# Regrouping a scan's chunks and re-issuing its transfers in a one-core hybrid decoder layer

## The chip, the core and the metric

The kernel runs on one core of a Trainium2 chip. Its time is the device time of one launch, in microseconds (us). A core has five engines with instruction streams of their own: TensorE (PE) for matmuls, VectorE (DVE), ScalarE (ACT), GpSimd (POOL) and SyncE (SP). SP, ACT and POOL also issue DMA transfers, in the order of their own streams.

## What is computed

One layer for two groups of tokens that share all weights: a prompt of 512 tokens and 8 sample tokens with caches of 2048 tokens, 520 columns in all. All data are 32-bit floats.

```python
x = x + 0.5 * swiglu_1(rmsnorm(x))                 # widths 1024, 2816
h = rmsnorm(x); u, q, k, v, ga, gb = split(h @ w_in)
# branch A: diagonal complex state space model, 64 groups of 16 channels, 64 states each
state[t] = abar * state[t-1] + bbar * u[t]         # chunked over time; samples: one step
y = gelu(Re(C state) + D * u); y_a = y * sigmoid(y @ w_glu)
# branch B: 3 groups of 4 heads, windows (128, 512, 2048), dilations (1, 4, 16), QK-norm, ALiBi,
#           groups mixed by their softmax denominators; samples attend to the caches
x = x + (sigmoid(ga) * (y_a @ w_proj_a) + sigmoid(gb) * (o_b @ w_proj_b)) @ w_out
x = x + 0.5 * swiglu_2(rmsnorm(x))
# results: x, the last states, and the key/value buffers moved on by one token
```

## The kernel before

Activations are kept transposed: a tile holds 128 channels by 520 tokens. Each product block multiplies one 128-column slice of a weight by all eight activation tiles. Operands are split into a high and a low part (`wsplit`, L165: ACT makes `wh`, DVE makes `wl`), and three products of the parts are summed, in two halves of 260 columns: 48 matmuls per block in `mm` (L212), all recorded at L221. Weights come one block at a time through `wfetch` (L169) from SP's queue into two raw buffers, three blocks ahead.

The layer runs as: first SwiGLU (bank ring `bigA`), the projection `w_in` as 42 blocks (ring `bigB`, two pairs of PSUM banks), eight GLU blocks, the output projections, second SwiGLU. The 42 blocks are two q/k blocks, eight u blocks, ten q/k blocks, six v blocks, sixteen gate blocks. Other work is threaded between them by generators. `pace()` (L746) is called after every block from the seventh u block on, counts them in `n`, takes steps of the scan in proportion (`SC` per block), and takes one step of each other generator when `n` reaches the next number in its list: `LV` leave, `NB` norms, `AT` attention, `KS` sample scores, `SM` samples, `YB` y blocks. Gate blocks are n = 19 to 34 and GLU blocks 35 to 42. The tool that places instructions also reorders within an engine by its own model of time; matmuls marked by `mark` keep their order.

The state space model treats four tokens as one column of a chunk. An u block is evicted by DVE with the norm factor (L797, L799) into `us`, stored to DRAM `uD` in four transfers (L802), and loaded back as `ut` (L648) with groups on the partitions. `entry` (L669) multiplies `ut` by the matrices `mp` (from DRAM `pD`, L662) into the chunk sums `XS` (ACT, L677), one quarter in each quarter of a product block, from the fourth u block on. `scan` (L684) then runs over `XS` in two halves of the groups. There are 128 columns in time order, 16 blocks of 8: a first pass sums each block over its 8 places, a second carries the state over the 16 blocks one after the other, a third fills the places. A step (`advance`) is four DVE operations, L701 to L704, on 512 elements per partition in the first and third pass and on 32 in the second. `leave` (L757) multiplies the states by output matrices (`qD`, and `ut` again), evicts them (ACT, L767) and stores `yD` from SP (L774). `y_block` (L1043) loads y back and makes the gelu with ACT and DVE in turn.

Norm factors of q and k are stored to `hD` and spread over partitions by SP (L850) for DVE's `normalise` (L852). `scores` (L1069) loads keys and a query row for each sample into one buffer, `spare`, which is taken out of the ring of three matrix buffers `mts`.

Of the kernel before, what the change touches and what calls it, by code (L numbers as in the profile page):

```python
# [21 lines left out]
NT = 520  # L22
# [17 lines left out]
EARLY = 2  # L40
ENTER = 2
RB = 7


SC = 1.85
LV = (21, 22, 22, 24, 25, 25, 26, 26)
NB = (16, 17, 17, 17, 18, 18, 19, 20, 21, 22, 22, 22, 22)
AT = (23, 24, 26, 27, 27, 28, 28, 29, 29, 30, 30, 31, 31, 31, 32, 32, 33, 35, 37)
KS = (22, 23, 23, 24, 26, 26, 27, 28)
SM = (31, 31, 36, 39, 39)  # L50
YB = (29, 29, 29, 29, 29, 31, 31, 33)
NL = 12
KV = 8
# [5 lines left out]
def build(tc, A):  # L59
# [575 lines left out]
    ssm = ExitStack()  # L635
    smp = pool(ssm, "smp")
    NH = NP // 2
    XS = [smp.tile([128, 2, NH, 145], F32, name=f"XS{h}") for h in range(2)]
    x0 = tmp("G")[:, 0:NP * 16].rearrange("p (r x) -> p r x", r=2)
    for ri, n in enumerate(("x0_re", "x0_im")):  # L640
        dma(x0[:, ri], A[n])
    for h in range(2):
        S.activation(XS[h][:, :, :, 0:8], x0.rearrange("p r (a b) -> p r a b", b=8)[:, :, h * NH:(h + 1) * NH], AF.Copy)
        V.memset(XS[h][:, :, :, 8:9], 0.0)

    def uload(u):
# [22 lines left out]
    def entry():  # L669
        for u in range(NP // 4):  # L670
            ut, mp = uload(u), mload(pD, u, dma)
            for a in range(4):
                p = u * 4 + a
                ps = bank()
                for ri in range(2):
                    mark(T.matmul(ps[:, ri], lhsT=mp[:, a * 2 + ri], rhs=ut[:, a, 8:CW], start=True, stop=True))  # L676
                S.activation(XS[p // NH][:, :, p % NH, 9:145], ps[:, 0:2], AF.Copy)  # L677
                yield
# [5 lines left out]
    def scan(h):  # L684
        X, pr = XS[h], slice(h * NH, (h + 1) * NH)
        sums = smp.tile([128, 2, NH, 16], F32, name="sums", tag="sums", bufs=2)

        def swap(x):
            return bass.AP(tensor=x.tensor, offset=x.offset + x.ap[1][0],
                           ap=[list(x.ap[0]), [-x.ap[1][0], 2]] + [list(d) for d in x.ap[2:]])  # L690

        def advance(out, W, x, add):
            n = 1 if len(x.shape) == 3 else x.shape[3]
            t1, t2 = (tmp(t)[:, 0:2 * NH * n] for t in "ST")
            w = [c[:, :, pr] for c in W]
            if n == 1:
                t1, t2 = (t.rearrange("p (r a) -> p r a", r=2) for t in (t1, t2))
            else:
                w = [c.unsqueeze(3).broadcast_to([128, 2, NH, n]) for c in w]
                t1, t2 = (t.rearrange("p (r a b) -> p r a b", r=2, b=n) for t in (t1, t2))  # L700
            V.tensor_tensor(t1, w[0], x, ALU.mult)  # L701
            V.tensor_tensor(t2, w[1], swap(x), ALU.mult)  # L702
            V.tensor_tensor(t1, t1, t2, ALU.add)
            V.tensor_tensor(out, add, t1, ALU.add)  # L704

        def at(j):
            return X[:, :, :, 8 + j:8 + j + 121:8]

        for j in range(1, 8):
            advance(sums, W4, sums if j > 1 else at(1), at(1 + j))  # L710
            yield
        for b in range(16):
            advance(X[:, :, :, 16 + 8 * b], W32, X[:, :, :, 8 + 8 * b], sums[:, :, :, b])
            if b % 2:
                yield
        for j in range(7):
            advance(at(j + 1), W4, at(j), at(j + 1))
            yield

        x0 = [X[:, ri, :, 0:8] for ri in range(2)]  # L720
        xn = [X[:, ri, :, 137:145] for ri in range(2)]
        t = tmp("S")[:, 0:8 * NH].rearrange("p (a b) -> p a b", b=8)
        ab = lambda ri: A1[:, ri, pr].unsqueeze(2).broadcast_to([128, NH, 8])
# [3 lines left out]
        o = tmp("G")[:, 0:18 * NH].rearrange("p (r a b) -> p r a b", r=2, b=9)  # L727
        S.activation(o, X[:, :, :, 136:145], AF.Copy)
        for ri in range(2):
            later(A["ostate"][ri][:, pr], o[:, ri])  # L730
        yield


    def scans():
        lo, hi = scan(0), scan(1)
        for order in ((lo,) * 7, (lo, hi) * 8, (lo, hi) * 7 + (hi,), (lo,), (hi,) * 8):
            for x in order:
                next(x, None)
                yield
# [6 lines left out]
    def pace(n=1):  # L746
        paced["n"] += n
        while paced["s"] < paced["n"] * SC:
            next(scanning, None)
            paced["s"] += 1  # L750
        for at, it in side:
            while at and at[0] <= paced["n"]:
                at.pop(0)
                next(it)


    def leave():  # L757
        for u in range(NP // 4):
            mt, ut, ps = mload(qD, u, later), uload(u), big()
            X, p0 = XS[u * 4 // NH], u * 4 % NH  # L760
            for a in range(4):
                p = p0 + a
                out = ps[:, a // 2, a % 2 * NC:(a % 2 + 1) * NC]
                mark(T.matmul(out, lhsT=mt[:, a * 3], rhs=X[:, 0, p, 0:NC], start=True, stop=False))
                mark(T.matmul(out, lhsT=mt[:, a * 3 + 1], rhs=X[:, 1, p, 0:NC], start=False, stop=False))
                mark(T.matmul(out, lhsT=mt[:, a * 3 + 2], rhs=ut[:, a, 0:NC], start=False, stop=True))
            S.activation(X[:, 0, p0:p0 + 4, 0:NC].rearrange("p (x a) b -> p x a b", x=2),  # L767
                         ps[:, :, 0:2 * NC].rearrange("p x (a b) -> p x a b", b=NC), AF.Copy)
            if u % 2 == 1:
                p = u * 4 - 4  # L770
                for g2 in range(2):
                    for t in range(4):
                        r0 = g2 * 64 + t * 16
                        dma(yD[p:p + 8, g2, :, t].rearrange("a k j -> k a j"), X[r0:r0 + 16, 0, p0 - 4:p0 + 4, 0:NC])  # L774
            yield
# [8 lines left out]
    for m in range(KB):  # L784
        ps = big()
        mm(ps, wnext(), n2.xs, between=entering if m > ENTER else None)
        u = us.next()

        for hf, c0, c1 in ((0, 0, 256), (0, 256, 260), (1, 260, 384), (1, 384, 512)):
            o = u[:, c0 // 128:(c1 + 127) // 128, 8 + c0 % 128:8 + (c1 - 1) % 128 + 1]  # L790
            src = ps[:, hf, c0 - hf * H:c1 - hf * H]
            r = R2[:, c0:c1]
            if c1 - c0 > 128:
                src, r = (x.rearrange("p (a b) -> p a b", b=128) for x in (src, r))
            else:
                o = o[:, 0]
            V.tensor_tensor(o, src, r, ALU.mult)  # L797
        for o in (u[:, 0, 0:8], u[:, 3, NC:CW]):
            V.tensor_tensor(o, ps[:, 1, 512 - H:520 - H], R2[:, 512:520], ALU.mult)  # L799
        for s in range(4):  # L800
            o = uD[m]
            dma(bass.AP(tensor=o.tensor, offset=o.offset + s * 16 * 4 * CW, ap=[[64 * 4 * CW, 2], [CW, 64], [1, CW]]), u[:, s])  # L802
        if m > 5:
            pace()
# [4 lines left out]
    def columns():  # L809
        for r in range(4):  # L810
            later(Rt[r * 32:r * 32 + 32, 0:4], rD[1, r * 128:r * 128 + 128].rearrange("(i a) -> a i", a=32))
        later(Rt[:, 4:8], rD[1, 0:512].rearrange("(r n) -> n r", r=4))

    for b in range(2, 12):
        qk_block(b, entering)
        if b == RB:
            with behind(qk[b]):
                columns()
        pace()
# [28 lines left out]
    def spread(b):  # L848
        for x in range(2):
            dma(norms[b % 2][x * 64:x * 64 + 64], hD[2 * b + x:2 * b + x + 1].broadcast_to([64, NT]))  # L850

# [204 lines left out]

    spare = mts.tiles.pop().rearrange("p a b -> p (a b)")
    sc = atp.tile([128, 3, 8, 4], F32, name="sc")
# [97 lines left out]

    side.append((list(AT), attending))
    side.append((list(KS), scores()))
    side.append((list(SM), samples()))
    yout = outputs()  # L1160
    for i in range(16):
        gate(i)
        if i == NL:
            assert not side[0][0] and next(scanning, None) is None and not side[3][0]
# [195 lines left out]
```

## Time and profile before

| | |
|---|---|
| median of three runs | 1318.41 us (1314.51 to 1320.13) |
| the profiled execution | 1321.28 us |
| its span, first to last instruction | 1319.5 us |
| busy in the span: PE, DVE, ACT, POOL | 96%, 56%, 33%, 8% |

The rows below come from the profiled execution and its times count from the start of its span. PE rows that pack together matmuls of one line show how many by "x". "Idle before" is the time for which an engine did nothing ahead of an instruction, and after the arrow stands what ended it, as far as the profile can tell.

### The profile page before, as it was taken

The numbers are of one execution on the slowest core, as the hardware profiler recorded it, in microseconds if no ns is written. First come the engines' busy times: TensorE is split into PE (matmuls) and PEld (weight loads), VectorE is DVE, ScalarE is ACT, GpSimd is POOL, SyncE is SP. The second block draws the span as 40 slices with busy tenths as digits, with TensorE's granted clock in tenths as the row PEclk, the third lists the DMA queues.
The fourth block names the chain that finished last, engine by engine and source line by source line (L and its number), as shares of the span: only waits on it lengthen the run. The fifth ranks groups of instructions, "written<-read, shape, count | busy, mean of one in ns | idle before, by whom it ended". The sixth has DMA issues, their size and how long they took to land.

```text
span 1319.5 us, 25222 instructions
## 1 busy us (share of the span) xinstructions
PE 1273.0 (96%) x10575; PEld 1245.5 (94%) x10575; DVE 739.3 (56%) x1268; ACT 430.8 (33%) x677; POOL 109.0 (8%) x211
## 2 busy tenths in 40 slices
PE   8999999999999878996989999999999999999999
PEld 7999999999999878996988899999999999999998
DVE  6794454535564238998944666775544334443442
ACT  5332232223343222332243653443332222222220
POOL 0110000000103001001330220000010000000000
PEclk9999999999999898998989899999999999999999
DMA  6674365546655445226786534556564426433332
GB/s 216 216 228 158 95 240 190 148 150 204 200 164 171 125 124 140 81 82 200 236 250 199 169 97 147 166 161 206 165 255 156 152 93 224 160 96 112 120 101 85
DMA packets 97401, 213.88 MB, mean 162 GB/s; under 512 B 37076, under 2 KB 53232, under 8 KB 96520
## 3 DMA queue, kind: packets, MB, share of 16 engines
q1 hardware_dynamic: 79096, 145.90, 36.2%
q0 software_dynamic: 7184, 60.01, 13.0%
q10 hardware_dynamic: 11008, 6.36, 1.8%
q8 instruction: 83, 1.36, 0.4%
q14 instruction: 30, 0.25, 0.1%
HBM read 188.72 MB, written 68.60 MB: 195 GB/s over the span
## 4 chain that ended last, share of the span: by engine, by line
PE 81%; DMA 8%; DVE 5%; issue 2%; SPq 2%; ACT 1%; POOL 0%; DVEq 0%; ACTq 0%; POOLq 0%
PE bigB L221 38%; PE bigA L221 28%; PE third L221 12%; DMA mt<-qkD 2%; DMA wr<-in_win 1%; DVE wl L167 1%; PE s L676 1%; DMA OB<-hD 1%; DMA uD<-us 1%; PE sb L953 1%; PE s L982 1%; DMA vt<-wD 1%; DVE t_T L702 1%; DMA mt<-in_kv 1%; DVE mt L1074 1%
## 5 line engine op out<-in xcount | busy, mean ns | idle before, releaser
L166 ACT ACTIVATE wh<-wr 128x1024 fp32r<-128x1024 f32 (+3 forms) x212 | 214.3, 1011 | 581.0 <-PE bigB L221 205.1
L167 DVE TENSOR_TENSOR wl<-wr,wh 128x1024 fp32r<-128x1024 f32 (+3 forms) x212 | 246.1, 1161 | 55.2 <-ACT wh L166 53.6
L221 PE MATMUL bigB<-xh,wh 128*128 128x260 f32 (+1 forms) x1216 | 254.4, 290 | 4.0 <-DVE us L799 3.7
L221 PE MATMUL bigB<-xl,wh 128*128 128x260 f32 (+1 forms) x1216 | 253.8, 288 | 0.4 <-DVE xl L302 0.4
L221 PE MATMUL bigB<-xh,wl 128*128 128x260 f32 (+1 forms) x1216 | 249.6, 286 | 0.0
L221 PEld LDWEIGHTS bigB<-xh,wh 128*128 128x128 f32 x1216 | 191.5, 192 | 6.1 <-DVE us L799 3.9
L221 PEld LDWEIGHTS bigB<-xl,wh 128*128 128x128 f32 x1216 | 192.1, 192 | 3.8 <-issue 3.2
L221 PEld LDWEIGHTS bigB<-xh,wl 128*128 128x128 f32 x1216 | 191.2, 192 | 0.7 <-issue 0.7
L221 PE MATMUL bigA<-xh,wh 128*128 128x260 f32 x704 | 143.4, 285 | 2.0 <-ACT xh L257 1.2
L221 PE MATMUL bigA<-xl,wh 128*128 128x260 f32 x704 | 142.7, 284 | 0.6 <-DVE xl L258 0.6
L221 PE MATMUL bigA<-xh,wl 128*128 128x260 f32 x704 | 142.2, 284 | 0.5 <-DVE wl L167 0.5
L221 PEld LDWEIGHTS bigA<-xh,wh 128*128 128x128 f32 x704 | 109.2, 190 | 4.3 <-ACT xh L257 2.9
L221 PEld LDWEIGHTS bigA<-xl,wh 128*128 128x128 f32 x704 | 108.8, 189 | 1.6 <-DVE xl L258 1.6
L221 PEld LDWEIGHTS bigA<-xh,wl 128*128 128x128 f32 x704 | 109.0, 189 | 0.7 <-DVE wl L167 0.7
L120 POOL COPY pace<-ah 1x1 f32<-1x1 f32 x48 | 19.9, 416 | 768.8 <-ACT ah L301 768.8
L221 PE MATMUL bigA<-ah,wh 128*128 128x260 f32 x352 | 71.2, 283 | 0.0
L221 PE MATMUL bigA<-al,wh 128*128 128x260 f32 x352 | 71.0, 283 | 0.0
L221 PE MATMUL bigA<-ah,wl 128*128 128x260 f32 x352 | 70.6, 282 | 0.0
L221 PE MATMUL third<-xh,wh 128*128 128x260 f32 x288 | 58.0, 282 | 0.0
L221 PE MATMUL third<-xh,wl 128*128 128x260 f32 x288 | 57.9, 283 | 0.0
L221 PE MATMUL third<-xl,wh 128*128 128x260 f32 x288 | 57.8, 282 | 0.0
L221 PEld LDWEIGHTS bigA<-ah,wh 128*128 128x128 f32 x352 | 54.2, 189 | 0.1
(386 smaller groups left out, 2045.6 us busy)
## 6 DMA issues: line engine op xcount, KB each, us to landing
out_okv<-in_kv POOLq DMA_DIRECT2D x32, 1023.5 KB, 6.2
wr<-in_wg SPq DMA_DIRECT2D x43, 512.0 KB
wr<-in_wu SPq DMA_DIRECT2D x43, 512.0 KB
wr<-in_win SPq DMA_DIRECT2D x42, 512.0 KB
wr<-in_wd SPq DMA_DIRECT2D x32, 448.0 KB
wr<-in_wd SPq DMA_DIRECT2D x16, 512.0 KB
out_okv<-in_kv POOLq DMA_DIRECT2D x8, 1022.0 KB, 6.0
ut<-uD POOLq DMA_DIRECT2D x16, 288.0 KB, 5.4
```

The costliest lines, as they stand in the source:

```text
L120: ins = G.tensor_copy(pace[0:1, 0:1], t[0:1, 0:1])
L166: S.activation(h, raw, AF.Copy)
L167: V.tensor_tensor(l, raw, h, ALU.subtract)
L221: i = T.matmul(ps[:, hf, 0:x.shape[1]], lhsT=a[:, c], rhs=x, start=k == 0 and j == 0, stop=k == n - 1 and j == 2)
L676: mark(T.matmul(ps[:, ri], lhsT=mp[:, a * 2 + ri], rhs=ut[:, a, 8:CW], start=True, stop=True))
L702: V.tensor_tensor(t2, w[1], swap(x), ALU.mult)
L953: T.matmul(o, lhsT=q[pr, qc], rhs=k[pr, kc], start=True, stop=True)
L982: T.matmul(po[x * 64:x * 64 + 64, l * 128:l * 128 + 128], lhsT=vt[:, kt, c:c + 64], rhs=pTs[x][:, j], start=j in (j0, 2), stop=j % 2 == 1)
L1074: V.tensor_tensor(qb, qb, kt, ALU.mult)
```

## The change

The 128 columns of `XS` are stored by place in the block instead of in time order, so that the 16 blocks' values of one place lie side by side; u is written to `us` in that order, and leave's eviction puts it back into time order. The scan uses one set of temporary tiles per half, its two halves alternate over other stretches, and both halves' end states are stored together afterwards (`states`, from SP). u's stores move from SP to POOL, the entry matrices from SP to ACT, the norm spreads and y's stores from SP to POOL, the token factors `Rt` from POOL to SP. Entry starts one u block later. The u products are cut at column 256. Scores use the rotating buffers `kvt`, as the samples do, and start only when the scan's memory has been given back, which comes two gates earlier. leave keeps all three matrix buffers. All lists of `pace` are new.

```diff
-ENTER = 2
+ENTER = 3
-SC = 1.85
-LV = (21, 22, 22, 24, 25, 25, 26, 26)
-NB = (16, 17, 17, 17, 18, 18, 19, 20, 21, 22, 22, 22, 22)
-AT = (23, 24, 26, 27, 27, 28, 28, 29, 29, 30, 30, 31, 31, 31, 32, 32, 33, 35, 37)
-KS = (22, 23, 23, 24, 26, 26, 27, 28)
-SM = (31, 31, 36, 39, 39)
-YB = (29, 29, 29, 29, 29, 31, 31, 33)
-NL = 12
+SC = 1.9
+LV = (21, 21, 22, 22, 27, 27, 28, 28)
+NB = (15, 15, 16, 16, 17, 17, 18, 18, 19, 19, 20, 20, 24)
+AT = (25, 26, 27, 28, 29, 30, 31, 32, 32, 33, 34, 34, 35, 35, 36, 36, 37, 38, 40)
+KS = (29, 30, 30, 31, 31, 32, 32, 33)
+SM = (34, 34, 37, 39, 40)
+YB = (29, 29, 30, 30, 31, 31, 32, 33)
+NL = 10
...
-    XS = [smp.tile([128, 2, NH, 145], F32, name=f"XS{h}") for h in range(2)]
+    XS = [smp.tile([128, 2, NH, 160], F32, name=f"XS{h}") for h in range(2)]
...
-            ut, mp = uload(u), mload(pD, u, dma)
+            ut, mp = uload(u), mload(pD, u, put)
...
-                S.activation(XS[p // NH][:, :, p % NH, 9:145], ps[:, 0:2], AF.Copy)
+                S.activation(X[:, :, i, 24:160], ps[:, 0:2], AF.Copy)
...
-        sums = smp.tile([128, 2, NH, 16], F32, name="sums", tag="sums", bufs=2)
+        sums, u1, u2 = (tmp(t)[:, 0:32 * n].rearrange("p (r a b) -> p r a b", r=2, b=16) for t in "GST")
...
         def at(j):
-            return X[:, :, :, 8 + j:8 + j + 121:8]
+            return X[:, :, :, 8 + 16 * j:24 + 16 * j]
         for j in range(1, 8):
-            advance(sums, W4, sums if j > 1 else at(1), at(1 + j))
+            advance(sums if j < 7 else at(8), W4, sums if j > 1 else at(1), at(1 + j))
             yield
         for b in range(16):
-            advance(X[:, :, :, 16 + 8 * b], W32, X[:, :, :, 8 + 8 * b], sums[:, :, :, b])
+            out = X[:, :, :, 9 + b] if b < 15 else X[:, :, :, 151]
+            advance(out, W32, X[:, :, :, 8 + b], X[:, :, :, 136 + b])
...
+    def states():
+        for h in range(2):
+            o = tmp("G")[:, 0:18 * NH].rearrange("p (r a b) -> p r a b", r=2, b=9)
+            S.activation(o, XS[h][:, :, :, 151:160], AF.Copy)
+            for ri in range(2):
+                dma(A["ostate"][ri][:, h * NH:(h + 1) * NH], o[:, ri])
...
-        for order in ((lo,) * 7, (lo, hi) * 8, (lo, hi) * 7 + (hi,), (lo,), (hi,) * 8):
+        for order in ((lo,) * 11, (lo, hi) * 12, (hi,) * 11):
...
-        while paced["s"] < paced["n"] * SC:
+        while paced["s"] < (paced["n"] - 1) * SC:
...
-            S.activation(X[:, 0, p0:p0 + 4, 0:NC].rearrange("p (x a) b -> p x a b", x=2),
-                         ps[:, :, 0:2 * NC].rearrange("p x (a b) -> p x a b", b=NC), AF.Copy)
+            for x in range(2):
+                o, r = X[:, 0, p0 + 2 * x:p0 + 2 * x + 2, 0:NC], ps[:, x, 0:2 * NC].rearrange("p (a b) -> p a b", b=NC)
+                S.activation(o[:, :, 8:NC].rearrange("p a (b j) -> p a b j", j=8),
+                             r[:, :, 8:NC].rearrange("p a (j b) -> p a b j", j=8), AF.Copy)
+            S.activation(X[:, 0, p0:p0 + 4, 0:8].rearrange("p (x a) b -> p x a b", x=2),
+                         ps[:, :, 0:2 * NC].rearrange("p x (a b) -> p x a b", b=NC)[:, :, :, 0:8], AF.Copy)
...
-                        dma(yD[p:p + 8, g2, :, t].rearrange("a k j -> k a j"), X[r0:r0 + 16, 0, p0 - 4:p0 + 4, 0:NC])
+                        later(yD[p:p + 8, g2, :, t].rearrange("a k j -> k a j"), X[r0:r0 + 16, 0, p0 - 4:p0 + 4, 0:NC])
...
-        mm(ps, wnext(), n2.xs, between=entering if m > ENTER else None)
+        mm(ps, wnext(), n2.xs, cut=256, between=entering if m > ENTER else None)
...
-            V.tensor_tensor(o, src, r, ALU.mult)
+        for sg in range(4):
+            V.tensor_tensor(u[:, sg, 8:NC].rearrange("p (j b) -> p b j", j=8),
+                            *(x.rearrange("p (b j) -> p b j", j=8) for x in
+                              (ps[:, sg // 2, sg % 2 * 128:sg % 2 * 128 + 128], R2[:, sg * 128:sg * 128 + 128])), ALU.mult)
...
-            dma(bass.AP(tensor=o.tensor, offset=o.offset + s * 16 * 4 * CW, ap=[[64 * 4 * CW, 2], [CW, 64], [1, CW]]), u[:, s])
+            later(bass.AP(tensor=o.tensor, offset=o.offset + s * 16 * 4 * CW, ap=[[64 * 4 * CW, 2], [CW, 64], [1, CW]]), u[:, s])
...
-            with behind(qk[b]):
-                columns()
+            columns()
...
-            dma(norms[b % 2][x * 64:x * 64 + 64], hD[2 * b + x:2 * b + x + 1].broadcast_to([64, NT]))
+            later(norms[b % 2][x * 64:x * 64 + 64], hD[2 * b + x:2 * b + x + 1].broadcast_to([64, NT]))
...
-    spare = mts.tiles.pop().rearrange("p a b -> p (a b)")
...
-            kt, qb = spare[:, 0:768], spare[:, 768:1536]
+            kt, qb = (sap.tile([128, 768], F32, name="kvt", tag="kvt", bufs=KV) for _ in range(2))
...
-    side.append((list(KS), scores()))
-    side.append((list(SM), samples()))
...
+            states()
             ssm.close()
...
+            side.append((list(KS), scores()))
+            side.append((list(SM), samples()))
             side.append((list(YB), yout))
```

## Rows read from the trace of the kernel before

**Rows 1.** The page's slices: 40 equal parts of the span, tenths busy or granted.
```profile
PE   8999999999999878996989999999999999999999
...
DVE  6794454535564238998944666775544334443442
...
PEclk9999999999999898998989899999999999999999
```

**Rows 2.** Windows: us, busy us per engine (instructions), PEclk, DMA share, GB/s.
```profile
428.00:520.00 92.00, 73.23 (x548) 71.26 (x547) 38.52 (x81) 22.91 (x44) 6.42 (x11) 0.89 0.45 127
...
520.00:606.00 86.00, 86.00 (x747) 83.09 (x746) 83.14 (x207) 32.41 (x63) 5.13 (x9) 1.00 0.31 92
606.00:618.00 12.00, 1.60 (x12) 1.39 (x11) 9.32 (x22) 0.96 (x5) 0.76 (x1) 0.71 0.79 264
618.00:730.00 112.00, 102.78 (x795) 96.14 (x794) 74.26 (x117) 39.57 (x84) 27.52 (x45) 0.94 0.75 223
730.00:840.00 110.00, 109.53 (x907) 101.32 (x906) 73.18 (x119) 57.70 (x117) 14.08 (x24) 0.97 0.48 141
840.00:1319.00 479.00, 476.22 (x3982) 475.67 (x3980) 218.90 (x277) 136.17 (x170) 19.30 (x46) 1.00 0.45 151
```

**Rows 3.** Timeline of PE, instructions that waited: start, us, what, idle before.
```profile
434.81 1.25 PE L676 MATMUL s<-ut,mt 128*128 128x136 f32 x4 [3.45 <-issue]
...
617.40 0.41 PE L886 MATMUL s<-ident,OB 128*48 128x128 f32 x1 [10.40 <-DVE OB L927]
```

**Rows 4.** Timeline of POOL, two loads.
```profile
448.80 0.54 POOL L648 DMA_DIRECT2D ut<-uD  x1 [9.29 <-DMA uD<-us]
...
505.72 1.53 POOL L662 DMA_DIRECT2D mt<-qD  x2
```

**Rows 5.** Chain of waits, 428 to 530 us: start, us, what.
```profile
447.06 0.46 PE s L676 x4
...
447.53 1.44 PE bigB L221 x12
...
482.64 8.46 DMA uD<-us
```

**Rows 6.** Timeline of SP's queue, one turn and the start of the next.
```profile
444.90 6.99 SPq L802 DMA_DIRECT2D uD<-us  x4
451.99 2.45 SPq L175 DMA_DIRECT2D wr<-in_win  x1
454.49 1.32 SPq L662 DMA_DIRECT2D mt<-pD  x2
455.91 7.58 SPq L802 DMA_DIRECT2D uD<-us  x4
```

**Rows 7.** DMA issues by line: queue, count, KB each, median us to landing.
```profile
ut<-uD POOLq DMA_DIRECT2D x16, 288.0 KB, 5.4
```

**Rows 8.** Line L544: ns min/median/max, first and last start, forms.
```profile
L544 ACTq DMA_DIRECT2D pD<-pst x32: 582/628/3950, 110.3 to 369.1; - x32
```

**Rows 9.** DVE groups, 398 to 850 us: busy us, mean ns | idle before.
```profile
L167 DVE TENSOR_TENSOR wl<-wr,wh 128x1024 fp32r<-128x1024 f32 x51 | 62.2, 1220 | 19.1 <-ACT wh L166 19.0
...
L703 DVE TENSOR_TENSOR t_S<-t_S,t_T 128x512 f32<-128x512 f32 x28 | 19.3, 689 | 0.2
...
L701 DVE TENSOR_TENSOR t_S<-W,XS 128x512 f32<-128x512 f32 x16 | 18.4, 1148 | 0.0
...
L704 DVE TENSOR_TENSOR XS<-XS,t_S 128x512 f32<-128x512 f32 x14 | 16.2, 1156 | 0.0
...
L1074 DVE TENSOR_TENSOR mt<-mt 128x768 f32<-128x768 f32 x8 | 7.7, 958 | 29.6 <-DMA mt<-qkD 22.0 <-DMA yD<-XS 7.6
...
L1050 DVE TENSOR_SCALAR t_T<-t_T 128x520 f32<-128x520 f32 x8 | 3.7, 462 | 9.9 <-ACT t_T L1049 9.9
```

**Rows 10.** Timeline of DVE, the memset of nq.
```profile
491.29 0.17 DVE L822 MEMSET nq<- 128x130 f32 x1 [14.13 <-DMA uD<-us]
```

**Rows 11.** ACT groups, 398 to 850 us: leave eviction.
```profile
L767 ACT ACTIVATE XS<-bigB 128x544 f32<-128x544 f32 x8 | 5.0, 620 | 10.5 <-PE bigB L766 8.2 <-DMA yD<-XS 2.4
```

More of the change, by code (lines that the diff above doesn't have):

```diff
@@ L644, in build, with place @@
         V.memset(XS[h][:, :, :, 8:9], 0.0)
+    def place(p):
+        return XS[p // NH], p % NH
     def uload(u):
@@ L676, in entry @@
                     mark(T.matmul(ps[:, ri], lhsT=mp[:, a * 2 + ri], rhs=ut[:, a, 8:CW], start=True, stop=True))
-                S.activation(XS[p // NH][:, :, p % NH, 9:145], ps[:, 0:2], AF.Copy)
+                X, i = place(p)
+                S.activation(X[:, :, i, 24:160], ps[:, 0:2], AF.Copy)
                 yield
@@ L684, in scan @@
     def scan(h):
-        X, pr = XS[h], slice(h * NH, (h + 1) * NH)
-        sums = smp.tile([128, 2, NH, 16], F32, name="sums", tag="sums", bufs=2)
+        X, n, pr = XS[h], NH, slice(h * NH, (h + 1) * NH)
+        sums, u1, u2 = (tmp(t)[:, 0:32 * n].rearrange("p (r a b) -> p r a b", r=2, b=16) for t in "GST")
         def swap(x):
@@ L692, in advance @@
         def advance(out, W, x, add):
-            n = 1 if len(x.shape) == 3 else x.shape[3]
-            t1, t2 = (tmp(t)[:, 0:2 * NH * n] for t in "ST")
             w = [c[:, :, pr] for c in W]
-            if n == 1:
-                t1, t2 = (t.rearrange("p (r a) -> p r a", r=2) for t in (t1, t2))
-            else:
-                w = [c.unsqueeze(3).broadcast_to([128, 2, NH, n]) for c in w]
-                t1, t2 = (t.rearrange("p (r a b) -> p r a b", r=2, b=n) for t in (t1, t2))
+            if len(x.shape) == 3:
+                t1, t2 = u1[:, :, :, 0], u2[:, :, :, 0]
+            else:
+                w = [c.unsqueeze(3).broadcast_to([128, 2, n, 16]) for c in w]
+                t1, t2 = u1, u2
             V.tensor_tensor(t1, w[0], x, ALU.mult)
@@ L720, in scan @@
         x0 = [X[:, ri, :, 0:8] for ri in range(2)]
-        xn = [X[:, ri, :, 137:145] for ri in range(2)]
-        t = tmp("S")[:, 0:8 * NH].rearrange("p (a b) -> p a b", b=8)
-        ab = lambda ri: A1[:, ri, pr].unsqueeze(2).broadcast_to([128, NH, 8])
+        xn = [X[:, ri, :, 152:160] for ri in range(2)]
+        t = u1.rearrange("p r a b -> p (r a b)")[:, 0:8 * n].rearrange("p (a b) -> p a b", b=8)
+        ab = lambda ri: A1[:, ri, pr].unsqueeze(2).broadcast_to([128, n, 8])
         for o, a, b, op in ((0, 0, 0, ALU.add), (0, 1, 1, ALU.subtract), (1, 0, 1, ALU.add), (1, 1, 0, ALU.add)):
@@ L726, in scan @@
             V.tensor_tensor(xn[o], xn[o], t, op)
[L727 to L730, printed above, removed]
         yield
+    def states():
[4 more added lines that the diff above has]
+                dma(A["ostate"][ri][:, h * NH:(h + 1) * NH], o[:, ri])
     def scans():
         lo, hi = scan(0), scan(1)
-        for order in ((lo,) * 7, (lo, hi) * 8, (lo, hi) * 7 + (hi,), (lo,), (hi,) * 8):
+        for order in ((lo,) * 11, (lo, hi) * 12, (hi,) * 11):
             for x in order:
@@ L759, in leave @@
             mt, ut, ps = mload(qD, u, later), uload(u), big()
-            X, p0 = XS[u * 4 // NH], u * 4 % NH
+            X, p0 = place(u * 4)
             for a in range(4):
@@ L785, in build @@
         ps = big()
-        mm(ps, wnext(), n2.xs, between=entering if m > ENTER else None)
+        mm(ps, wnext(), n2.xs, cut=256, between=entering if m > ENTER else None)
         u = us.next()
[L789 to L796, printed above, removed]
-            V.tensor_tensor(o, src, r, ALU.mult)
+        for sg in range(4):
+            V.tensor_tensor(u[:, sg, 8:NC].rearrange("p (j b) -> p b j", j=8),
+                            *(x.rearrange("p (b j) -> p b j", j=8) for x in
+                              (ps[:, sg // 2, sg % 2 * 128:sg % 2 * 128 + 128], R2[:, sg * 128:sg * 128 + 128])), ALU.mult)
         for o in (u[:, 0, 0:8], u[:, 3, NC:CW]):
-            V.tensor_tensor(o, ps[:, 1, 512 - H:520 - H], R2[:, 512:520], ALU.mult)
+            V.tensor_tensor(o, ps[:, 1, 256:264], R2[:, 512:520], ALU.mult)
         for s in range(4):
             o = uD[m]
-            dma(bass.AP(tensor=o.tensor, offset=o.offset + s * 16 * 4 * CW, ap=[[64 * 4 * CW, 2], [CW, 64], [1, CW]]), u[:, s])
+            later(bass.AP(tensor=o.tensor, offset=o.offset + s * 16 * 4 * CW, ap=[[64 * 4 * CW, 2], [CW, 64], [1, CW]]), u[:, s])
         if m > 5:
@@ L810, in columns @@
         for r in range(4):
-            later(Rt[r * 32:r * 32 + 32, 0:4], rD[1, r * 128:r * 128 + 128].rearrange("(i a) -> a i", a=32))
-        later(Rt[:, 4:8], rD[1, 0:512].rearrange("(r n) -> n r", r=4))
+            dma(Rt[r * 32:r * 32 + 32, 0:4], rD[1, r * 128:r * 128 + 128].rearrange("(i a) -> a i", a=32))
+        dma(Rt[:, 4:8], rD[1, 0:512].rearrange("(r n) -> n r", r=4))
     for b in range(2, 12):
@@ L1163, in build @@
         if i == NL:
-            assert not side[0][0] and next(scanning, None) is None and not side[3][0]
+            assert not side[0][0] and next(scanning, None) is None
+            states()
             ssm.close()
```

## The prediction, made before the change was run

> **What bounds the kernel now.** I read the slices first, then the windows by stage, then, for the two places where TensorE stands still, the idle rows of PE and the chain of waits; last the queues that the chain names.
>
> The slices show two different kernels [rows 1]. For the first 398 us and from 840 us on PE is full at the full clock, and nothing here touches that. In the middle, where all edits lie, PE dips, its clock dips, and DVE reaches 9 tenths. The windows give sizes [rows 2]. I price a stretch's loss as PE's idle time plus (1 - granted clock) x its busy time, which is an estimate, since the clock column is a mean. 428 to 520 us: 18.8 us idle + 0.11 x 73.2 = 26.8 us. 520 to 606: nothing. 606 to 618: 10.4 + 0.5 = 10.9 us. 618 to 730: 9.2 + 6.2 = 15.4 us. 730 to 840: 0.5 + 3.3 = 3.8 us. That is 57 us in all: no schedule of the same matmuls gets more than that.
>
> The idle rows tell who is late. From 428 to 520 PE stops seven times, six of them at the entry matmuls of L676 (the first stands in [rows 3]), at the head of a block and for 1 to 4 us: their input, `ut`, has not landed. The profile calls it "issue"; POOL's row shows the load waiting for the store, 9.3 us [rows 4]. An undisturbed block there is 4 x (1.44 + 0.46) = 7.6 us of PE [rows 5]. But SP needs a turn of 11.0 us per block, from 444.90 to 455.91: 7.0 for u's four stores, 2.5 for a weight tile, 1.3 for the two entry-matrix loads [rows 6]. So SP, not PE, sets the pace of these blocks; the stores are the largest part of its turn, a store's data lands 8.5 us later [rows 5], and only then may POOL issue the load that PE waits for (5.4 us to landing, [rows 7]). The one stop of 10.4 us at 617.40 is another matter: a transpose waits for DVE L927, a tiny operation that stands in a DVE queue that has been 83.1 of 86 us busy [rows 2, 3].
>
> **The change, part by part.**
>
> *u's stores to POOL, entry matrices to ACT, entry one block later.* SP loses 7.0 + 1.3 of its 11.0 us per block; 2.5 is left, so it no longer sets the pace. POOL gains four stores per block at 0.55 each, if they cost what its `ut` loads cost (0.54, [rows 4]): 2.2, with its load 2.8 us of a 7.6 us block. ACT gains two issues of 0.63 [rows 8], 1.3 us per block, where it was 22.9 of 92 us busy [rows 2]: hidden, and if that cover went, 10 us over eight blocks. The new chain from a block's end to `ut`: eviction about 1.2, stores 2.2, landing between 5.4 (the POOL row) and 8.5 (the SP row), load 0.6 + 5.4: 15 to 18 us. Entry in block m > 3 instead of m > 2 asks for it three blocks and a little later: 3 x 5.75 + 1.4 = 18.7 us for the first (48 matmuls of 0.12, the rate of the last window in [rows 2]), 24 later. So it fits, with little to spare at first. From the 26.8 us I keep 3 for stops that stay: **24 us gained**; bounds 14 (stores land late, half the stops stay) and 27. Cutting the product at 256 keeps 520 columns, and the four strided evictions on DVE replace four of the same length: at worst twice the time, as strided against dense in [rows 9], half a us per block on a DVE that was 38.5 of 92 busy: hidden.
>
> *Chunks by place.* A scan step over 512 elements reads or writes XS every eighth element: 1.15 us, against 0.69 for the dense L703 of the same shape [rows 9]. In the new layout the sixteen elements lie side by side, so I take 0.69. That touches 32 multiplies and 28 adds (L701, L702, L704): 60 x 0.46 = 27.5 us of DVE (nothing, if a run of sixteen costs like a stride). It is not 27.5 us of time. By the end of the v blocks, where PE's 10.4 us stop stands, the scan is some 32 of 46 steps along, the first pass of both halves and most of one half's third: I put 16 of the 27.5 as saved by then. But PE also arrives sooner: most of the first part's 24 us falls behind u's last block, where the scan begins, and I put 17 of them. What helps is the 14.1 us during which DVE stood behind one memset for u's store [rows 10]; a store on an unclogged queue lands perhaps 8 us sooner. The backlog then goes from 10.4 to 10.4 + 17 - 16 - 8 = 3 us. Of the 10.9 I take **6 us gained**; bounds 0 and 11.
>
> *Norm spreads and y's stores to POOL, columns and states to SP.* 24 + 32 issues at 0.55 = 31 us of POOL in the 302 us from 428 to 730, where it was busy 40 [rows 2, 4]: no time of its own, but a load behind a waiting POOL instruction is late. SP's weight loads stand behind fewer others. I count zero, with 2 us either way inside the bounds above.
>
> *Scores and samples later, in rotating buffers; leave with a third matrix buffer.* Each score waited for its keys in one buffer: DVE stood 29.6 us on them in eight scores [rows 9]. Now four scores are in flight, but they move from the early gates to gates 10 to 14, where y's blocks are also made. I add up DVE there, over six gates: eight scores at 2 x 0.96 = 15.3, eight y blocks of one operation of 0.46 and three of 0.69 = 20, seven attention items of two 512-element operations at 0.69 = 9.7, seven weight splits at 1.22 = 8.5 [rows 9]: 54 us, against 6 x 5.75 = 34.5 us of the gates' products and, if attention's matmuls between them add half as much (an estimate), 52 us of PE. DVE is full there and the loss moves rather than goes. leave's eviction becomes three ACT instructions for one of 0.62 [rows 11], at most 1.2 us more per block on an ACT that is 39.6 of 112 busy: hidden. Of the 19.2 us lost from 618 to 840 I take **2 us gained**, bounds 14 gained and 20 lost.
>
> Sum: 24 + 6 + 2 = 32. The profiled execution took 1321.3 us (1.8 around its span); 1289.3. The runs' median is 2.9 below that execution, so the forecast is **1287 us**.
>
> **A rule weighed against the stores.** POOL's issues near 505 us, with DVE full, take no longer than the one at 448.80 with DVE idle: 0.77 each for the two matrix loads, 0.54 for `ut` [rows 2, 4]. The Trainium skill (SBUF — State Buffer, "SBUF: two separate sides") warns that DMAs issued from POOL can starve: POOL writes their descriptors through a port that DVE locks in some of its modes; a later place on that page reports a transfer that went from about 0.62 to 3.1 us. At that price four stores and a load would hold POOL for some 13 us per block against SP's turn of 11.0 today, and part one would cost some 16 us over eight blocks in place of its gain. No row here shows it; a milder form of it is the first rival.
>
> **Rivals.**
> - *The stores are no quicker on POOL.* If POOL's issues are held up, by DVE or by a full queue, until they cost what SP's did, four stores take 7.0 and land 8.5 later; with the load the chain is 23 us against 18.7 to 24, and POOL's turn 7.6 is just the block. Half the stops stay: 14 instead of 24 gained, and 4 lost on late spreads: 32 - 14 = 18, 1301. For it: the same bytes, in the same small pieces, and the page's rule above points this way. Against: the DMA engines were 0.45 busy there and POOL's issues kept their 0.5 to 0.8 [rows 2, 4].
> - *POOL puts u's load behind younger stores (the slower side).* If the load for block m stands behind the stores of block m-1, then each block pays 1.2 + 2.2 + 0.6 + 5.4 = 9.4 us less the 1.4 before the first entry matmul, 8.0 us of idle; a low clock adds some 2.7 (at the resumption 0.46 becomes 1.25, [rows 3, 5], and the next products pay too). Five blocks (four of u, one of qk): 53 us against the 26.8 lost now: 26 us worse, less the 8 of the other parts: 1336. It decides from 7 us per block on: 5 x 7 = 26.8 + 8. Against it: POOL's order before is not the written one; leave's first matrix loads (qD) go out at 505.72 [rows 4], though the code that writes them runs at the third gate.
> - *Gates 10 to 15 become DVE's.* Waits of 29.6 for scores and 9.9 for y's ACT partner [rows 9] no longer fall into empty DVE time: 39.5 us, plus 2 of work over room, against the 19.2 lost today: 22 worse in place of 2 better, which leaves 30 - 22 = 8 of the gain: 1310, and 1315 with a low clock after such stops. I count it as no change. Against: four scores in flight.
> - *All of it works*, and the gates keep their 14: 27 + 10 + 14 = 51, 1268.
>
> **How the numbers follow.** Forecast 0.52, all works 0.20, stores no quicker 0.13, gates full 0.07, POOL order 0.08. Half a per cent, 6.6 us, is about what a measurement tells from no change: faster below 1312, slower above 1325. The forecast, "all of it works" and the slow stores are faster (0.85 together), the full gates no change (0.07), the POOL order is slower (0.08). The range runs from 1265 to 1311: it leaves out the last two cases (0.15) and the far ends of the others.
>
> **What would show it.** Right: SP's turn per block near 3 us; entry stops of L676 under 5 us in all from 428 on; qk 5 some 24 us earlier; L701 and L704 at 0.69 for 512 elements; the stop before L886 under 5 us; DVE at 9 tenths in the gates after leave. Wrong: POOL rows of 1.5 us and more for uD, PE idle at L676 with POOL waiting for DVE, strided prices still at 1.15, or PE idle at the head of the GLU blocks for ys.

## The result, and the profile after

The changed kernel takes 1279.7 us (median of 4 runs, 1277.1 to 1281.3) against 1316.5 us for the one before, measured beside it: ratio 0.972, 95% interval 0.968 to 0.976, 36.8 us less. The forecast was 1287 in a range from 1265 to 1311. The profiled execution took 1280.84 us, its span 1279.0, which is 40.5 below the span of before. One execution that took 4907 us, of the kernel "before, u's stores on POOL" below, is left out of its numbers.

The slices of the kernel after, to be laid beside [rows 1]:

```profile
PE   8999999999999999998999999999999999999999
...
DVE  6794455635555339988436768765544334434442
...
PEclk9999999999999999999999889999999999999999
```

The two dips of PE in the middle of before have gone but for one 8, and of the low clock two slices are left, from about 703 to 767 us. The windows say the same in us (columns as in [rows 2]):

```profile
428.00:520.00 92.00, 90.42 (x779) 88.17 (x778) 58.74 (x144) 32.21 (x58) 32.72 (x44) 1.00 0.59 157
...
580.00:620.00 40.00, 34.61 (x288) 33.55 (x287) 32.20 (x64) 11.03 (x26) 21.98 (x40) 1.00 0.83 254
620.00:700.00 80.00, 80.00 (x673) 76.16 (x673) 32.71 (x50) 35.67 (x83) 28.99 (x50) 1.00 0.71 210
700.00:760.00 60.00, 54.76 (x412) 46.95 (x411) 47.60 (x79) 37.05 (x80) 11.58 (x19) 0.86 0.57 183
```

Priced as in the prediction (idle time plus the part of the clock that was not granted), 428 to 520 us loses 1.6 us, where [rows 2] gave 26.8. The rest of the middle loses 5.4 (580 to 620) and 5.2 + 0.14 x 54.8 = 12.9 (700 to 760), where it was 10.9 + 15.4 + 3.8 = 30.1. So 57 became 20: 37 us, of which 25 in u's blocks.

The idle rows of PE (timeline, instructions that waited over 1 us):

```profile
446.26 0.70 PE L681 MATMUL s<-ut,mt 128*128 128x136 f32 x4 [1.58 <-issue]
...
582.09 0.29 PE L893 MATMUL s<-ident,OB 128*48 128x128 f32 x1 [1.60 <-DVE OB L934]
...
599.68 0.50 PE L772 MATMUL bigB<-XS,mt 128*128 128x136 f32 x2 [2.18 <-ACT t_sq L886]
...
705.16 0.43 PE L989 MATMUL s<-pT,vt 128*64 128x128 f32 x2 [1.81 <-ACT pT L981]
...
726.02 0.44 PE L980 MATMUL s<-ident,p 128*128 128x128 f32 x2 [1.17 <-ACT p L975]
...
738.04 0.50 PE L1121 MATMUL s<-ident,L 32*128 32x32 f32 x3 [2.04 <-DVE L L1117]
```

One of the six stops at the entry matmuls is left (L681 is the old L676). The transposition of v's last columns (L893, the old L886) waits 1.60 us in place of 10.40 [rows 3], and it comes at 582.09, not at 617.40. From there to the end of the span it takes 696.9 us after and 702.1 before. So 35.3 of the 40.5 us are won ahead of this one instruction, and I use its time below to tell roughly where each experiment gains or loses.

### The profile page after: what moved, and what is told of

Read it like the earlier page. It is cut to its first block, busy times and chain, and to the rows that moved or that the text cites. A ratio compares the mean times of both kernels' runs of the same rounds, so it can differ in the third digit from the quotient of the medians.

```text
span 1279.0 us, 25230 instructions
## 1 busy us (share of the span) xinstructions
PE 1258.8 (98%) x10575; PEld 1234.1 (96%) x10575; DVE 714.8 (56%) x1268; ACT 434.7 (34%) x695; POOL 161.0 (13%) x289
## 4 chain that ended last, share of the span: by engine, by line
PE 91%; DMA 4%; issue 1%; SPq 1%; POOL 1%; ACT 1%; DVE 0%; ACTq 0%; POOLq 0%; DVEq 0%
PE bigB L221 44%; PE bigA L221 29%; PE third L221 13%; PE s L681 1%; DMA kvt<-qkD 1%; PE s L989 1%; DMA ut<-uD 1%; PE sb L960 1%; DMA vD<-tok 1%; DMA gD<-t_sq 0%; PE s L980 0%; DMA x<-in_xT 0%; DMA wr<-in_wg 0%; PE bigB L774 0%; DMA OB<-hD 0%
## 5 line engine op out<-in xcount | busy, mean ns | idle before, releaser
L221 PE MATMUL bigB<-xh,wh 128*128 128x260 f32 (+1 forms) x1216 | 249.1, 286 | 0.3 <-ACT wh L166 0.3
L221 PE MATMUL bigB<-xl,wh 128*128 128x260 f32 (+1 forms) x1216 | 248.7, 284 | 0.0
L221 PE MATMUL bigB<-xh,wl 128*128 128x260 f32 (+1 forms) x1216 | 246.9, 284 | 0.0
L221 PEld LDWEIGHTS bigB<-xl,wh 128*128 128x128 f32 x1216 | 188.1, 188 | 2.4 <-issue 2.4
L221 PEld LDWEIGHTS bigB<-xh,wh 128*128 128x128 f32 x1216 | 187.6, 189 | 1.6 <-issue 0.5
L221 PEld LDWEIGHTS bigB<-xh,wl 128*128 128x128 f32 x1216 | 187.9, 188 | 0.9 <-issue 0.9
L221 PE MATMUL bigA<-ah,wh 128*128 128x260 f32 x352 | 71.2, 283 | 0.0
```

The costliest lines, as they stand in the source:

```text
L221: i = T.matmul(ps[:, hf, 0:x.shape[1]], lhsT=a[:, c], rhs=x, start=k == 0 and j == 0, stop=k == n - 1 and j == 2)
```

## Experiments

Twelve kernels. "In us" is the ratio times 1316.5, the median of before in the first comparison, so that runs from several chips stand on one scale; after is 0.972, 1279.7. "v's last" is the start of the transposition just named.

| kernel | ratio (95%) | in us | v's last | from there to the end |
|---|---|---|---|---|
| before | 1 | 1316.5 | 617.4 | 702.1 |
| after | 0.972 (0.968 to 0.976) | 1279.7 | 582.1 | 696.9 |
| after, u's stores on SP | 0.984 (0.981 to 0.987) | 1295.9 | 597.5 | 698.8 |
| after, entry a block sooner | 0.980 (0.978 to 0.983) | 1290.5 | 597.1 | 694.5 |
| after, chunks in time order | 0.984 (0.982 to 0.987) | 1295.7 | 595.5 | 698.5 |
| before, u's stores on POOL | 0.994 (0.992 to 0.997) | 1309.0 | 606.1 | 696.1 |
| before, stores and entry | 0.983 (0.981 to 0.985) | 1294.1 | 591.2 | 699.5 |
| before, chunks by place | 0.997 (0.995 to 0.999) | 1312.4 | 603.9 | 699.5 |
| after, one score at a time | 0.975 (0.971 to 0.979) | 1282.9 | 582.0 | 703.8 |
| after, spreads, y, entry matrices on SP | 0.977 (0.973 to 0.980) | 1285.7 | 579.6 | 705.0 |
| after, v's store later | 0.973 (0.969 to 0.976) | 1280.5 | 579.0 | 694.0 |
| after, y earlier, scores later | 0.971 (0.969 to 0.973) | 1278.3 | 580.9 | 696.8 |
| after, attention earlier | 0.970 (0.966 to 0.974) | 1276.9 | 580.5 | 693.8 |
| after, all three edits | 0.968 (0.965 to 0.972) | 1274.9 | 582.1 | 692.8 |

The last two columns are of one profiled execution each, which can lie some us from its median (7 us in "before, chunks by place"). The tool that places instructions orders them anew for every build. The first experiment has the order of after on PE, DVE and ACT, ACT's loads of entry matrices apart, and the second that of before but for one memset. "v's store later" came out with the order of after on every engine, so it is after measured once more: the two spans lie 6.0 us apart, and the last two columns 3 us each. In the others a few us may come from the order.

**u's stores back on SP.**

```diff
 for s in range(4):
-    later(...uD..., u[:, s])
+    dma(...uD..., u[:, s])
```

> The kernel after, with one thing undone: u's four stores per block are issued by SP again (entry one block later, entry matrices on ACT, chunks by place and all orders stay). My theory: SP's turn goes from 2.5 to 7.0 + 2.5 = 9.5 us per block of 7.6 us of TensorE, so SP sets the pace of u's blocks again; 1.9 us late for each of eight blocks, and stops at the entry matmuls that cost more than that by the clock: 12 to 20 us slower than after, 1292 to 1300. Rival (the gain of this stage comes from the later entry and the emptier SP alone, the place of the stores is nothing): within 3 us of after, 1277 to 1283.

Measured: 16.2 us slower than after, as my theory had it. SP's queue in this kernel (timeline of SP):

```profile
417.62 3.58 SPq L810 DMA_DIRECT2D uD<-us  x4
...
433.13 7.08 SPq L810 DMA_DIRECT2D uD<-us  x4
440.31 2.50 SPq L175 DMA_DIRECT2D wr<-in_win  x1
442.90 6.79 SPq L810 DMA_DIRECT2D uD<-us  x4
```

A turn is 442.90 - 433.13 = 9.8 us, 9.5 expected. In after SP has nothing but weight tiles to issue in that stretch (timeline of SP):

```profile
420.76 106.93 SPq L175 DMA_DIRECT2D wr<-in_win  x16
```

As PE, DVE and ACT keep the order of their instructions, this is the place of the stores alone.

**Only the stores on POOL, in the kernel before** (the reverse edit there).

> The kernel before, with one thing done: u's four stores per block are issued by POOL. My theory: SP's turn falls from 11.0 to about 4 us, below the block's 7.6, so most of the 26.8 us between 428 and 520 us comes back; the first entry of each block still comes one block sooner than in after, so a few stops stay: 15 to 20 us faster than before, 1297 to 1302. Rival (the later entry is what removes the stops): under 5 us faster, 1312 to 1317.

Measured: 7.5 us faster, half of the least that I expected, and above what the rival allowed. POOL's timeline shows why, first in this kernel, then in after:

```profile
444.48 3.24 POOL L802 DMA_DIRECT2D uD<-us  x4
454.08 0.58 POOL L648 DMA_DIRECT2D ut<-uD  x1 [6.36 <-PE s L676]
454.66 3.20 POOL L802 DMA_DIRECT2D uD<-us  x4
464.12 0.58 POOL L648 DMA_DIRECT2D ut<-uD  x1 [6.27 <-DMA uD<-us]
464.70 3.19 POOL L802 DMA_DIRECT2D uD<-us  x4
474.44 0.58 POOL L648 DMA_DIRECT2D ut<-uD  x1 [6.55 <-DMA uD<-us]
```

```profile
440.24 0.59 POOL L653 DMA_DIRECT2D ut<-uD  x1 [4.43 <-DMA uD<-us]
440.82 3.20 POOL L810 DMA_DIRECT2D uD<-us  x4
...
452.98 0.59 POOL L653 DMA_DIRECT2D ut<-uD  x1 [4.30 <-PE s L681]
453.56 3.20 POOL L810 DMA_DIRECT2D uD<-us  x4
460.62 0.59 POOL L653 DMA_DIRECT2D ut<-uD  x1 [3.85 <-PE s L681]
```

With stores and load in one queue, the early entry puts each block's load right behind that block's own four stores, and POOL stands at it until they have landed (6.27 and 6.55 us in the rows; the first load's wait ended with a buffer that TensorE freed). The next block's stores stand behind the load. A turn is 3.2 + 6.5 + 0.6 = 10.3 us (464.12 to 474.44), against a block of 7.6. SP no longer sets the pace, POOL does. In after the load stands one set of stores further back. From 452.98 on, what it reads has landed by its turn, and it waits for TensorE to free the buffer: a turn of 7.6 us (452.98 to 460.62).

**The same from the other side: after with the entry a block sooner.**

```diff
-ENTER = 3
+ENTER = 2
```

> The kernel after, with entry one block sooner (ENTER 2 as in before; stores on POOL, all else as in after). My theory, formed on the run with only the stores moved: POOL then gets each block's ut load ahead of the next block's four stores, and waits at it for the landing of the stores before, so its turn is 3.2 of stores + 6.5 of landing + 0.6 = 10.3 us per block against TensorE's 7.6; the later entry is what turns this order round. 10 to 17 us slower than after, 1290 to 1297. Rival (my prediction's reading: the later entry only gives a chain of 15 to 18 us some 5 us more room, so without it the first stops alone come back): 2 to 5 us slower, 1282 to 1285.

Measured: 10.9 us slower than after, inside my theory's numbers and outside the rival's. POOL's loads come at 454.26, 464.62 and 474.97, 10.3 us apart, and PE stops 6.05 us at an entry matmul at 445.53. One of the loads, behind POOL's wait for the landing (timeline of POOL):

```profile
464.62 0.59 POOL L653 DMA_DIRECT2D ut<-uD  x1 [6.58 <-DMA uD<-us]
```

**Stores and entry together, in the kernel before.** The last scan step of the second half comes here after leave has overwritten the first columns of that half, so its end states are made from other values; the instructions are the same.

```diff
-ENTER = 2
+ENTER = 3
-    dma(...uD..., u[:, s])
+    later(...uD..., u[:, s])
-        while paced["s"] < paced["n"] * SC:
+        while paced["s"] < (paced["n"] - 1) * SC:
```

> The kernel before, with u's stores on POOL and entry one block later (and the scan's first step one gate later, which the later entry needs), entry matrices still on SP, chunks in time order, all else as before. My theory: the two together remove the stops of 428 to 520 us, where the stores alone removed a third; SP keeps 2.5 + 1.3 of 7.6 us; but DVE's strided scan is then the one that is late at the last transposes of v, so 15 to 22 us faster than before, 1293 to 1300, with a stop of about 10 us left there. Rival (the entry matrices on SP hold the blocks too): under 10 us faster, 1305 or more.

Measured: 22.4 us faster than before, at the upper end of what I expected. Of the stops at the entry matmuls one of 0.77 us is left, and the one at v's last stays, as long as before (10.40 there; PE timeline of this kernel):

```profile
591.23 0.41 PE L886 MATMUL s<-ident,OB 128*48 128x128 f32 x1 [10.77 <-DVE OB L927]
```

So the entry matrices may stay on SP, and stores and entry are to be made together: 7.5 for the stores alone, 22.4 for both. The later entry alone was not run in the kernel before; in the first experiment, which has it with the stores on SP, TensorE stops four times at the entry matmuls, for 0.9 to 3.7 us.

**Chunks by place alone, in the kernel before** (layout, scan and the eviction of u and of leave as in after; queues, entry, lists and the order of the halves as before).

> The kernel before, with the chunks kept by place alone (queues, entry and orders as before). My theory: DVE saves 27 us of busy time, but the 14 to 16 us of stops at the entry matmuls stay, so only the lag before L886 (10.4 us) and a little behind it can come back: 3 to 11 us faster than before, 1306 to 1313. Rival (DVE's strided scan is what the middle of the kernel waits for): 20 us faster or more, 1297 or less.

Measured: 4.1 us faster (interval 2.0 to 6.1). The stops at the entry matmuls stay, for example this one in its PE timeline, beside the one at 434.81 in [rows 3]:

```profile
433.22 1.22 PE L676 MATMUL s<-ut,mt 128*128 128x136 f32 x4 [3.59 <-issue]
```

In its profiled execution the stop at v's last is gone, and three of 1.3 to 4.4 us stand between 620 and 637 us, at attention's first products and at a transposition.

**Chunks in time order, in the kernel after** (the scan reads every eighth column again; all else as in after).

> The kernel after, with the chunks in order of time again (the scan reads every eighth element; queues and all orders as in after). My theory: DVE has 27 us more to do between 470 and 600 us, PE arrives at the last transposes of v as early as in after, and waits there for DVE: the stop of 1.6 us becomes 10 to 18 us, and the kernel is 8 to 20 us slower than after, 1288 to 1300. Rival (the sixteen-long runs cost DVE like the stride, or DVE has room): within 3 us of after.

Measured: 16.1 us slower than after. Nearly the same edit is worth 4 us in the kernel before and 16 in the kernel after. DVE's groups, first in this kernel, then in after (columns as in [rows 9]):

```profile
L705 DVE TENSOR_TENSOR t_S<-W,XS 128x512 f32<-128x512 f32 x16 | 18.6, 1161 | 0.1
...
L708 DVE TENSOR_TENSOR XS<-XS,t_S 128x512 f32<-128x512 f32 x14 | 16.5, 1181 | 0.1
```

```profile
L708 DVE TENSOR_TENSOR XS<-XS,t_S 128x512 f32<-128x512 f32 x16 | 11.0, 686 | 0.1
L705 DVE TENSOR_TENSOR t_S<-W,XS 128x512 f32<-128x512 f32 x16 | 11.0, 686 | 0.1
```

A run of sixteen costs the dense price, 0.686 us, the one assumed. The late DVE reaches TensorE by two ways in this kernel (timelines of PE and of ACT):

```profile
582.43 1.11 PE L923 MATMUL s<-ident,t_sq 128*128 128x128 f32 x4 [7.60 <-ACT t_sq L920]
...
595.50 0.39 PE L886 MATMUL s<-ident,OB 128*48 128x128 f32 x1 [3.97 <-DVE OB L927]
```

```profile
580.49 0.45 ACT L736 ACTIVATE t_G<-XS 128x288 f32<-128x288 f32 x1 [10.90 <-DVE XS L730]
```

ACT waits 10.9 us to copy the end states of the scan, and v's eviction stands behind that copy; this, not the transposition that waits for DVE itself, is the longer stop. The two together are 11.6 us, where after has 1.6. The copy stands so only in the kernel after, which stores both halves' end states together, so part of the 16 us belongs to that arrangement.

**One score at a time**, in the kernel after.

```diff
-    kt, qb = (sap.tile(..., name="kvt", tag="kvt", bufs=KV) for _ in range(2))
+    kt = sap.tile(..., name="kvt", tag="kvt", bufs=KV)
+    qb = sap.tile(..., name="qb1", tag="qb1", bufs=1)
```

> The kernel after, with the scores' query rows in a single buffer of their own (one ring buffer fewer for the rest), so that a score waits until the one before it is done with it; places and all else as in after. My theory, from the prediction: the waits of 3.7 us per score of before return, now in gates 10 to 14 where DVE is full, 20 to 30 us of DVE idle; 4 to 15 us slower than after, 1284 to 1295. Rival (only the new places matter, the buffers are worth nothing): within 2 us of after.

Measured: 3.3 us slower by the ratios, whose intervals overlap, so unclear; the profiled span is 6.8 longer, all of it behind v's last, and two executions of one order differ by 6.0 above. DVE's row of the scores, first in this kernel, then in after:

```profile
L1081 DVE TENSOR_TENSOR qb<-qb,kvt 128x768 f32<-128x768 f32 x8 | 7.7, 958 | 9.3 <-DMA qb<-qkD 7.1 <-DMA kvt<-in_kv 2.1
```

```profile
L1080 DVE TENSOR_TENSOR kvt<-kvt 128x768 f32<-128x768 f32 x8 | 7.6, 952 | 2.3 <-DMA kvt<-qkD 2.3
```

9.3 us of waits, where I expected 20 to 30. That the buffers in flight are worth anything isn't shown.

**Spreads, y's stores and the entry matrices back on SP**, in the kernel after (`later` to `dma` in `spread` and `leave`, `put` to `dma` in `entry`).

> The kernel after, with the norm spreads, y's stores and the entry matrices issued by SP again (u's stores stay on POOL). My theory: these three moves are worth nothing by themselves; SP has 2.5 + 1.3 of 7.6 us per block to do: within 3 us of after, 1277 to 1283. Rival (weight tiles stand behind them on SP, and TensorE waits for weights or for leave's buffers): 4 us slower or more, 1284 or more.

Measured: 6.0 us slower; the intervals overlap a little, so it isn't shown to be slower. The stops are not behind weights:

```profile
598.54 0.80 PE L960 MATMUL sb<-qk 64*128 64x128 f32 x4 [5.11 <-ACT qk L908]
...
601.57 0.80 PE L960 MATMUL sb<-qk 64*128 64x128 f32 x4 [2.23 <-DVE qk L863]
```

In this build attention's first products (L960) stand in TensorE's stream at 598.5, in after at 612.3, while DVE normalises its inputs only some 4 us sooner than in after. So PE's order changed with the queues, and the run doesn't settle what the three places are worth by themselves.

**What is left between 700 and 755 us: three tries, and all of them together.** The 1.5 MB store of v's tile moved behind the ninth gate; y's blocks earlier with scores and samples later; attention earlier, one item to a gate.

```diff
-    later(A["ovt"]..., vt)            # after the last v block
+        if i == 8: later(A["ovt"]..., vt)   # in the loop over the gates
...
-KS = (29, 30, 30, 31, 31, 32, 32, 33)
-SM = (34, 34, 37, 39, 40)
-YB = (29, 29, 30, 30, 31, 31, 32, 33)
+KS = (30, 31, 31, 32, 32, 33, 33, 34)
+SM = (35, 36, 37, 39, 40)
+YB = (29, 29, 29, 30, 30, 30, 31, 31)
...
-AT = (25, 26, 27, 28, 29, 30, 31, 32, 32, 33, 34, 34, 35, 35, 36, 36, 37, 38, 40)
+AT = (22, 23, 24, 25, 26, 27, 28, 29, 30, 31, 32, 33, 34, 35, 36, 36, 37, 38, 40)
```

> The kernel after, with the 1.5 MB store of v's tile to its output issued after the ninth gate and not behind the last v block. My theory: the two stops of 0.8 us at the ut loads near 610 us and the late landings there (9.7 us) go: 1 to 3 us faster than after. Rival (TensorE's other work hides it anyway): within 1 us of after.

> The kernel after, with y's blocks earlier in the gates (places 29 29 29 30 30 30 31 31), scores and samples one place later each. My theory: what is left between 700 and 755 us (5 us of stops and 7 by the low clock) comes from y's last block, for which the first GLU block waits while TensorE has only attention's small products; with y done two gates sooner the GLU's products fill that stretch: 3 to 8 us faster than after, 1271 to 1277. Rival (DVE's sum of work in gates 10 to 15 sets it, whatever the order): within 2 us of after, the stops elsewhere.

> The kernel after, with attention's items from place 22 on, one to a gate, and one double place in place of four (22 to 36, 36, 37, 38, 40). My theory: what is left between 700 and 755 us is the small products of attention, two items to a gate, whose links through DVE and ACT TensorE waits for; y's earlier blocks did nothing for it. Between 620 and 700 us DVE is 0.4 busy, so the items fit there: 4 to 12 us faster than after, 1268 to 1276. Rival (the samples and y set that stretch, or attention now waits for the scans and leave): within 2 us of after, or slower.

> The kernel after, with attention from place 22 on as in the run above, the store of v's tile after the ninth gate, and y's blocks earlier and scores later by a place or two. My theory: the small gains add up: 5 to 14 us faster than after, 1266 to 1275. Rival: what attention earlier gives alone, or less where these moves crowd the same queues.

Measured: 0.8 us slower and 1.4, 2.8 and 4.8 us faster than after, all with intervals that overlap that of after: none is shown to be faster. The first edit changed nothing: the tool that places instructions put the store of v back between the same neighbours in POOL's stream (timelines of POOL, first after, then this run):

```profile
586.28 0.80 POOL L938 DMA_DIRECT2D out_ovt<-vt  x1
```

```profile
582.31 0.80 POOL L1167 DMA_DIRECT2D out_ovt<-vt  x1
```

So that theory is untested. What the run does show is how far two executions of one order lie apart: between 575 and 625 us `ut` lands in 9.1 us (median) in after and in 5.0 here, and the two stops near 610 are not there. In the last run the store stands in its old place too (586.08), so "all three edits" is attention and y earlier. TensorE's idle time between 700 and 760 us is 5.2 us in after and 6.1, 6.0, 5.8 and 5.6 in the four runs: none of them shortened it, only the places of the stops changed. With y earlier the stop in attention stays; with attention earlier it goes, and one at the high part of y comes; with both a shorter one is left. One PE row of each:

```profile
726.70 0.44 PE L980 MATMUL s<-ident,p 128*128 128x128 f32 x2 [1.17 <-ACT p L975]
```

```profile
731.72 0.80 PE L221 MATMUL bigB<-yh,wh 128*128 128x260 f32 x2 [4.22 <-ACT yh L304]
```

```profile
736.84 0.51 PE L221 MATMUL bigB<-yh,wh 128*128 128x260 f32 x2 [2.07 <-ACT yh L304]
```

In the second of these, ACT's making of y's high part (L304) stands right behind the samples' softmax (L1115), which waited for DVE and a load of 6.5 us. Attention, y and the samples each have a chain of their own through that stretch, and taking one out shows the next. The last run has the lowest time of the study, 0.968 of before; it isn't told apart from after's 0.972.

## Why the prediction was right, step by step

- **What bounds u's blocks.** Right: SP's turn. After, SP issues nothing but weights in that stretch, one stop of 1.58 us is left in place of six, and the part gained 25.2 us for 24. The step under it was only half seen. I costed POOL's share by its sum (2.8 us of a 7.6 us block) and took the later entry for a matter of slack in a chain of 15 to 18 us. The runs show that it is a matter of order: with the load right behind its own stores POOL's turn is 10.3 us, and of the 22.4 us that stores and entry give together the stores alone give 7.5. So the size of the term was right on reasoning that missed why the later entry is needed. Of the rival "POOL puts u's load behind younger stores" the order came true and the harm didn't: in after younger stores do stand ahead of each load, and that is what lets the older ones land.
- **A POOL store costs 0.55.** Too low: four take 3.20 us, 0.80 each. With the load that is 3.8 of 7.6 us, and still hidden.
- **The stores are no quicker on POOL** (rival): refuted. Four take 3.2 us there with DVE 59 of 92 us busy, against about 7 on SP in the first experiment. The rule of the Trainium skill (SBUF — State Buffer, "SBUF: two separate sides") that made this rival heavier doesn't show here: no four stores took more than 3.4 us on POOL. Whether DVE ran in one of the modes that the rule means, no run shows.
- **Chunks by place.** Right in price (0.686 us against the 0.69 assumed). The account of the lag, 10.4 + 17 - 16 - 8 = 3 us before v's last transposition, came out near the 1.60 that was seen, but in part by luck. Stores and entry without the new layout are the case for which it gives 19 us; the stop there is 10.77. TensorE was ready for that transposition 26.5 us sooner than before (580.5 after 607.0), and DVE reached it 26.2 us sooner too (591.2 after 617.4). So the terms 17 and 8, 9 us together, came to 0.4; of the 8, DVE's wait behind u's store fell by 4 (14.1 to 10.1). The term of 16 was too large as well: DVE reaches the transposition in after 9.1 us sooner than in that run, and 13.4 sooner than with the chunks in time order. These errors cancel. By its stage the term was 6 us, and 9.3 measured (10.9 to 1.6). That the layout is worth 4 us in the kernel before and 16 in the kernel after is measured; that DVE had time while SP held TensorE back is argued. Against it, DVE is as late in before (10.40) as behind the mended queues (10.77), and part of the 16 comes by ACT's copy of the end states.
- **DVE full in gates 10 to 15.** The size is right (2 us gained forecast; 19.2 to 5.4 - 1.6 + 12.9 = 16.7 by the same pricing, 2.5), the cause only in part. DVE is full from 700 to 720 us (19.9 of 20 us busy), but only 13.2 and 14.5 of 20 in the two stretches behind it, where TensorE's granted clock is 0.69 and 0.89. What TensorE waits for there are chains of small products through ACT and DVE, as the rows of the last runs show. As these stops were not forecast, that the size agrees is luck in part. The third rival (DVE the bound of the gates, 22 us worse) is refuted: the scores' waits fell from 29.6 to 2.3 us and nothing took their place in size.
- **Spreads, y's stores and entry matrices at nothing.** For the entry matrices it stands (the stages of 428 to 520 us are as full with them on SP: 71.2 of 72 us between 428 and 500, after 70.4). For spreads and y's stores it isn't settled.

The sum by stage: 25.2 + 9.3 + 2.5 = 37.0 against 32, where the medians differ by 36.8 and the two profiled executions by 40.5. The 7 us between forecast and median are these 5 us, and 2 of the base: the forecast started from 1318.4, the median of three runs, and the comparison, with a fourth, has 1316.5 for the same kernel.

## What to carry to other kernels

Where a store and the load that reads it back share a queue, a sum of issue times doesn't tell the pace: look at what stands right ahead of the load, and put one later set of stores between, so that the landing is hidden. An engine's saving is not a saving of time: nearly the same 27.5 us of DVE gave 4 us in one kernel and 16 in the other, so price the rest again after each stage is mended. Before an experiment with a moved transfer is read, look whether the transfer moved: here the placing tool undid one. Small dependent products of several branches in one stretch show one stop each in turn; moving one branch uncovers the next.

## What the runs showed of the hardware

The same store (72 KB) cost SP some 1.75 us of issue (7.0 for four, [rows 6]) and POOL 0.80. SP's price is not fixed: in the first experiment the first four stores, with nothing ahead of them in the listing for 2 us, took 3.58 us together, the next six sets 6.3 to 7.5 us, and the last, 5.8 us behind SP's issue before it, 5.1. What holds SP up isn't shown, but a price read from a busy queue doesn't hold for another. DVE reads and writes runs of sixteen elements out of a row at the dense price, 0.686 us for 512 elements per partition, and every eighth element at 1.15 to 1.18. One order of instructions, executed twice (after and "v's store later"), took spans of 1279.0 and 1273.0 us, with a granted clock of 0.69 and 0.83 between 720 and 740 us.
